# Memory cross-attention in float16 parts, its heads as generators, its output by pairs of heads

## The chip, the core and the metric

The kernel runs on one core of one Trainium2 chip. A core has five engines with instruction streams of their own: PE (TensorE, matrix multiplications; its weight loads are listed as PEld), DVE (VectorE), ACT (ScalarE), POOL (GpSimd) and SP (SyncE, which here issues most of the DMA transfers). Each stream is worked off in order, and an instruction waits for semaphores that other engines or transfers raise. The metric is the device time of one execution, in microseconds (us), as the median of repeated runs.

## What is computed

A trunk of two layers runs over 512 tokens of width 1024. Each layer has a mixing part (an RWKV-7 branch, a sparse-attention branch and gates, then one output projection `w_out`), a cross-attention into 256 memory tokens, and a feed-forward part: a SwiGLU in layer 0, eight experts of which each token takes two in layer 1 (MoE).

```python
x = x + memory_attention(rms_norm(x, norm_mem[l]), rms_norm(mem, mem_tok_norm[l]), mem_wq[l], ...)
h = rms_norm(x, norm_ffn[l])
# memory_attention: four heads of 128
q = rms_norm((h @ wq).reshape(bsz, seqlen, MEM_HEADS, MEM_HEAD_DIM), q_norm)
k = rms_norm(k.reshape(bsz, n_mem, MEM_HEADS, MEM_HEAD_DIM), k_norm)
s = jnp.einsum('bshd,bmhd->bhsm', q, k).astype(jnp.float32) * (MEM_HEAD_DIM ** -0.5)
p = jax.nn.softmax(s, axis=-1).astype(v.dtype)
```

Then p times v, and the heads side by side times `mem_wo`. The change touches this attention in both layers, and the step from it to the experts.

## The kernel before

Matrices are multiplied as pairs of float16 parts: a float32 operand a is split into hi (a cast to float16) and lo (a minus hi, in float16), and a product is three passes, hi·hi, lo·hi and hi·lo, added up in PSUM. `wtile` (L249 to L270) does this for a piece of weights of 512 KB: a DMA into a buffer `raw` on SP's queue (L259), the cast `whi` on ACT (L264), the rest `wlo` on DVE (L269). The buffers rotate in a pool set up with a number of raw, hi and lo buffers. `norm_T` (L182 to L202) normalises the four token tiles of 128 (square and sum on ACT L182, `rs` on DVE L164 and POOL L165, scaling on DVE L187), transposes them on PE (L193) and splits them (cast on ACT L201, lo on DVE L202). `proj_feat` (L286) and `proj_first` (L298) give outputs with features on the partitions, `proj_tok` (L328) with tokens on the partitions.

`mem_attn` (L1151 to L1217) takes the four heads one after the other: a projection `pf`, a copy `aqT` and a square of it, sums `pss`, scores `pms` (L1190), softmax (`amx`, exp into `apr`, its sum, and `apr` scaled at L1203), transposes `pmt` (L1209), and `pmo` (L1215), the product with v. The scores and `pmo` are float32 products there, of one pass each in the code, and `pmo` alone is split, into `oh` and `ol`. When all heads are there, `resid` (L1087 to L1093) multiplies by `mem_wo` in two halves of 512 columns over all four heads and adds to x. The keys and values of the memory tokens (`mem_kv`, L1106 to L1148) are made ahead: those of layer 0 at the start of the program, those of layer 1 inside the attention of layer 0, by the table `KV`, and kept in DRAM as `kTd` and `vd` in float32.

The weights of `w_out`, of the attention and of the FFN of layer 0 share one pool. The order of instructions on every engine comes from a scheduler that moves instructions of the text past one another where the data allow it; on SP it sets in which order the loads are issued. After `w_out` of layer 0, DVE's queue also holds seven small rows that prepare constants of layer 1's RWKV branch (`mu`, `w`, `a`, `kc`), which wait for DMAs of a few KB that stand behind the weight loads on SP.

In layer 1 the attention is followed by `norm_T` with rows that are kept (`row`), the splits `rowh` (ACT, L1281) and `rowl` (POOL, L1282), the router (transposes, `eh` and `el`, logits `plog`, then the choice on DVE) and the experts. Their first splits, `ewhi` (ACT, L1516) and `ewlo` (DVE, L1517), stand in the queues among the router's work. The experts' weights, 2 MB at a time, go into `eraw`, of which the pool `moeraw` holds four.

## Time and profile before

| what | us |
|---|---|
| median of 3 runs (lowest, highest) | 2107.54 (2106.56, 2109.30) |
| the profiled execution | 2112.5 |
| its span in the trace | 2110.7 |
| the stages in the trace: `w_out` of layer 0 | 524 to 566.3 |
| attention 0, with the keys and values of layer 1 | 566.3 to 669.6 |
| FFN of layer 0 | 669.6 to 1016 |
| mixing of layer 1, and its `w_out` | 1016 to 1553 |
| attention 1 | 1553 to 1629.9 |
| norm and router | 1629.9 to 1675 |
| experts | 1675 to 2098 |

The profiled execution was 5.0 us longer than the median, and 1.8 us of its time lie around the span. The page gives the busy time of the engines over the whole span (PE 93%) and in 40 slices. Stages differ, so the trace was read stage by stage: the busy time of each engine and the granted clock of TensorE in each stretch, and then, in order of time, what each engine did and what ended each idle time. The clock has two levels, 2.4 GHz (written 1.00) and 1.2 GHz (0.50). A busy time of one matmul in these rows reaches to its modelled end; how long PE needs for a row of matmuls is read from where the next ones start.

### The profile page before, as it was taken

To read this page: it belongs to the slowest core of one execution; us is meant where nothing else is said; L and a number is where in the kernel's file an instruction comes from. 1 tells how busy PE (TensorE), PEld (TensorE's weight loads), DVE (VectorE), ACT (ScalarE), POOL (GpSimd) and SP (SyncE) were. 2 spreads that over 40 slices of the span, in tenths; PEclk is the share of its full clock that TensorE was granted. 3 is DMA by queue.
4 is the path that set the end of the run, shared out by engine and by line. 5 is a ranking of instruction groups with operands and counts; after the bars stand their busy time and mean duration, and the time that the engine had idled before them with its cause. 6 is when DMAs were issued, how large, how long until landed. Compare 5 with 4: busy or idle time off the path is not lost.

```text
span 2110.7 us, 40673 instructions
## 1 busy us (share of the span) xinstructions
PE 1959.2 (93%) x16712; PEld 1291.7 (61%) x16712; DVE 1403.1 (66%) x2338; ACT 1018.8 (48%) x1641; POOL 343.5 (16%) x358
## 2 busy tenths in 40 slices
PE   7998899899999999999999888979998699999997
PEld 4664466364555444444583546536454699999996
DVE  6776987747655333322578997574755688888887
ACT  5543345443444333322543444543343588888883
POOL 2260601003000000000251350100200310000002
PEclk9998899979999999999999998988999799999998
DMA  7343424425551333333334332443544599999994
GB/s 230 104 98 78 120 68 127 107 79 164 170 150 50 110 100 100 102 107 101 117 82 98 80 114 63 110 103 110 165 129 171 164 377 372 352 353 345 346 348 135
DMA packets 346709, 332.51 MB, mean 158 GB/s; under 512 B 101889, under 2 KB 263809, under 8 KB 346514
## 3 DMA queue, kind: packets, MB, share of 16 engines
q1 hardware_dynamic: 335408, 306.03, 46.5%
q10 hardware_dynamic: 8482, 15.39, 2.0%
q0 software_dynamic: 2624, 8.40, 1.1%
q8 instruction: 133, 2.18, 0.4%
q14 instruction: 62, 0.51, 0.1%
HBM read 297.05 MB, written 32.72 MB: 156 GB/s over the span
## 4 chain that ended last, share of the span: by engine, by line
PE 68%; DVE 14%; DMA 6%; issue 3%; ACT 3%; SPq 2%; POOL 2%; ACTq 0%; DVEq 0%; POOLq 0%
PE pf L286 22%; PE pe L1534 11%; PE ptok L328 10%; PE py L1579 6%; PE pSy L901 3%; PE pf L298 2%; PE ptok L346 2%; DVE wlo L269 1%; DVE iacc L515 1%; DVE pr L1000 1%; DVE m L514 1%; PE psc L524 1%; ACT whi L264 1%; PE pp L555 1%; PE pA L805 1%
## 5 line engine op out<-in xcount | busy, mean ns | idle before, releaser
L264 ACT ACTIVATE whi<-raw 128x1024 f16<-128x1024 f32 (+3 forms) x242 | 227.2, 940 | 446.4 <-PE pf L286 193.4
L269 DVE SCALAR_TENSOR_TENSOR wlo<-raw,whi 128x1024 f16<-128x1024 f32 (+3 forms) x208 | 232.5, 1119 | 206.2 <-ACT whi L264 201.0
L1517 DVE SCALAR_TENSOR_TENSOR ewlo<-eraw,ewhi 128x1024 f16<-128x1024 f32 x265 | 321.1, 1221 | 61.9 <-ACT ewhi L1516 51.9
L286 PEld LDWEIGHTS <-whi 128*128 128x128 f16 x1888 | 184.5, 100 | 236.2 <-issue 39.2
L1516 ACT ACTIVATE ewhi<-eraw 128x1024 f16<-128x1024 f32 x265 | 277.5, 1053 | 80.6 <-PE py L1579 33.4
L1534 PE MATMUL pe<-XT,ewhi 128*128 128x144 f16 x2816 | 208.4, 227 | 2.4 <-issue 2.4
L1534 PEld LDWEIGHTS <-ewhi 128*128 128x128 f16 x2816 | 185.0, 98 | 3.6 <-issue 3.1
L286 PE MATMUL pf<-hh,whi 128*128 128x512 f16 x448 | 173.4, 387 | 2.4 <-ACT gt L1047 1.1
L286 PE MATMUL pf<-hl,whi 128*128 128x512 f16 x448 | 173.4, 387 | 0.0
L286 PEld LDWEIGHTS <-wlo 128*128 128x128 f16 x944 | 91.8, 99 | 112.8 <-issue 12.0
L286 PE MATMUL pf<-fh,whi 128*128 128x512 f16 x336 | 127.3, 379 | 0.0
L286 PE MATMUL pf<-fl,whi 128*128 128x512 f16 x336 | 127.3, 379 | 0.0
L1534 PE MATMUL pe<-XT,ewlo 128*128 128x144 f16 x1408 | 117.9, 227 | 1.0 <-issue 1.0
L286 PE MATMUL pf<-hh,wlo 128*128 128x512 f16 x448 | 113.4, 385 | 0.0
L267 POOL TENSOR_TENSOR wlo<-raw,whi 128x1024 f16<-128x1024 f32 (+3 forms) x34 | 58.5, 1721 | 288.5 <-ACT raw L266 199.1
L1579 PE MATMUL py<-HT,ewhi 128*128 128x144 f16 x1408 | 103.0, 226 | 0.1
L165 POOL TENSOR_TENSOR rs<-rs,nrm_e 128x1 f32<-128x1 f32 x28 | 16.8, 601 | 519.7 <-DVE rs L164 519.7
L1534 PEld LDWEIGHTS <-ewlo 128*128 128x128 f16 x1408 | 94.7, 98 | 1.6 <-issue 1.6
L1579 PEld LDWEIGHTS <-ewhi 128*128 128x128 f16 x1408 | 91.6, 98 | 0.3 <-issue 0.2
L286 PE MATMUL pf<-fh,wlo 128*128 128x512 f16 x336 | 79.4, 379 | 0.0
L346 PE MATMUL ptok<-whi,hh 128*128 128x256 f16 (+1 forms) x320 | 75.1, 275 | 2.1 <-ACT qe L482 2.0
L346 PE MATMUL ptok<-whi,hl 128*128 128x256 f16 (+1 forms) x320 | 75.1, 275 | 0.0
(459 smaller groups left out, 3934.2 us busy)
## 6 DMA issues: line engine op xcount, KB each, us to landing
raw<-in_w_in_dram SPq DMA_DIRECT2D x76, 512.0 KB
eraw<-in_moe_wg_dram SPq DMA_DIRECT2D x16, 2048.0 KB
eraw<-in_moe_wu_dram SPq DMA_DIRECT2D x16, 2048.0 KB
eraw<-in_moe_wd_dram SPq DMA_DIRECT2D x16, 2048.0 KB
eraw<-in_moe_wg_dram SPq DMA_DIRECT2D x8, 1536.0 KB
eraw<-in_moe_wu_dram SPq DMA_DIRECT2D x8, 1536.0 KB
eraw<-in_moe_wd_dram SPq DMA_DIRECT2D x8, 1536.0 KB
raw<-in_ffn_wg_dram SPq DMA_DIRECT2D x22, 512.0 KB
```

What stands on the lines that cost most here:

```text
L264: nc.scalar.activation(hi, raw, AF.Copy, scale=SW)
L267: nc.gpsimd.tensor_tensor(lo, raw, hi, OP.subtract)
L269: nc.vector.scalar_tensor_tensor(lo, raw, SW, hi, OP.mult, OP.subtract)
L286: self.nc.tensor.matmul(p, lhsT=w[:, k, :], rhs=x[k], start=first, stop=last)
L298: m = self.nc.tensor.matmul(ps[i][:, cs], lhsT=w[:, k, :], rhs=x[k][:, cs], start=hf == 0 and start, stop=stop, skip_group_check=True)
L328: mm(ps[t][:, :N], lhsT=x[:, k0 + k, ts], rhs=w[:, k, :], start=k0 == 0 and first, stop=k0 + kg == kt and last)
L346: mm(p, lhsT=x[:, k0 + k, ts], rhs=w[:, k, :], start=k0 == 0 and t % 2 == 0 and first, stop=k0 + kg == kt and last, skip_group_check=True)
L901: m = mm(p[e][:, cc % 4, jj, :], lhsT=l, rhs=r, start=first[e] is None, stop=x == (1 if cc else 0), skip_group_check=True)
L1516: a = nc.scalar.activation(r[0], w, AF.Copy, scale=SW)
L1517: d = nc.vector.scalar_tensor_tensor(r[1], w, SW, r[0], OP.mult, OP.subtract)
L1534: mm(p[:, i * n:(i + 1) * n], lhsT=w[:, k, :], rhs=XT[:, k, h, :], start=z == 0, stop=z == len(ms) - 1)
L1579: mm(ps[d], lhsT=w[:, i, d * P:(d + 1) * P], rhs=HT[:, k, h, :], start=k == 0 and w is wh and h == 0 and d % per == 0, stop=k == FT - 1 an ...
```

## The change

In `mem_attn`: queries, keys, values and probabilities are split into float16 parts, so that each score block is three passes of 128x256 where it was one float32 product, and `pmo` six passes of 128x512 where it was two float32 products. The splits are a cast on ACT and a subtraction on DVE each, where one copy stood; `kTd` and `vd` hold both parts. Each head is a generator with a pause in the middle; the second half of head h is written behind the first half of head h+2. The product with `mem_wo` is made for heads 0 and 1 and then for heads 2 and 3, so x is added to twice as often. The attention has a weight pool of its own (three raw, three hi, three lo), opened over free space, and `hold` orders its loads behind the last load of `w_out`. The normalised input lies in one tile with the tag "hl", no longer also in "hh". For the experts, the fourth raw buffer is a pool of its own; the router's split rows are allocated ahead of the row tiles; the last tile's `rowl` is on DVE, and its `rowh` is ordered behind the last `eh`.

```diff
     def split_ps(self, hi, lo, p, scale=None):
...
-            nc.scalar.copy(hi, p)
+            self.marks["hi"] = nc.scalar.copy(hi, p).ins
...
             self.lastw = nc.sync.dma_start(raw[:, :, o:o + n], pc.rearrange("(k p) c -> p k c", p=P)).ins
+            if self.hold:
+                self.order(self.lastw, self.hold)
...
-        hh = self.hp.tile([P, KT, SEQ], F16, name="qh", tag="hh", bufs=1)
-        hl = self.hp.tile([P, KT, SEQ], F16, name="ql", tag="hl", bufs=1)
-        self.norm_T(x, NT, [(I["norm_mem"][l], hh, hl)])
-        with tc.tile_pool(name="mattn", bufs=1, reuse_waits="tile") as mp:
+        hq = self.hp.tile([P, 2, KT, SEQ], F16, name="qhl", tag="hl", bufs=1)
+        hh, hl = hq[:, 0], hq[:, 1]
+        with self.more_weights(3, 3, 3), tc.tile_pool(name="mattn", bufs=1, reuse_waits="tile") as mp:
...
-                nc.vector.tensor_copy(qT, pq)
+                self.split_ps(qT[:, 0, :], qT[:, 1, :], pq, self.SM / SW)
...
-                        nc.tensor.matmul(psc[:, i * 256:(i + 1) * 256], lhsT=qT[:, t * P:(t + 1) * P], rhs=kT[:, h, :],
-                                         start=True, stop=True)
+                        for z, (a, b) in enumerate(three):
+                            nc.tensor.matmul(psc[:, i * 256:(i + 1) * 256], lhsT=qT[:, a, t * P:(t + 1) * P], rhs=kT[:, b, h, :],
+                                             start=z == 0, stop=z == 2)
...
-                for mt in range(2):
-                    nc.tensor.matmul(po, lhsT=v[:, mt, h * P:(h + 1) * P], rhs=pT[:, mt, :], start=mt == 0, stop=mt == 1)
-                self.split_ps(oh[:, h, :], ol[:, h, :], po)
-            self.resid(I["mem_wo"][l], oh, ol, x, 4)
+                    self.split_ps(pT[mt][:, 0, :], pT[mt][:, 1, :], pp, self.SP)
+                po = self.sm("pmo")
+                for z, (mt, (a, b)) in enumerate(itertools.product(range(2), ((0, 0), (0, 1), (1, 0)))):
+                    nc.tensor.matmul(po, lhsT=v[:, b, mt, h * P:(h + 1) * P], rhs=pT[mt][:, a, :], start=z == 0, stop=z == 5)
+                self.split_ps(oh[:, h, :], ol[:, h, :], po, 1 / (self.SM * self.SP))
+                yield
+            def output(pair, hf, kg=2):
+                hs, ks = slice(hf * 512, hf * 512 + 512), slice(2 * pair, 2 * pair + 2)
+                ps = self.proj_tok([I["mem_wo"][l][pair * 256:pair * 256 + 256, hs]], oh[:, ks, :], ol[:, ks, :], NT, 2, kg=kg)
+                for t in range(NT):
+                    nc.vector.scalar_tensor_tensor(x[:, t, hs], ps[t], 1 / SW, x[:, t, hs], OP.mult, OP.add)
+            wq = lambda h: I["mem_wq"][l][:, h * P:(h + 1) * P]
+            hs = [head(h, pq) for h, pq in enumerate(self.proj_first([wq(0), wq(1)], hk, lk))]
+            for g in hs:
+                next(g)
+            next(kv, None)
+            for h in (2, 3):
+                hs.append(head(h, self.proj_feat(wq(h), hk, lk)))
+                next(hs[h - 2])
+                next(hs[h])
+                for _ in range(2 if h == 2 else 0):
+                    next(kv, None)
+            output(0, 0)
+            next(hs[2])
+            output(0, 1)
+            next(hs[3])
+            output(1, 0, 1)
+            output(1, 1)
...
                 for t, r in enumerate(rows):
-                    self.marks["rows"] = nc.scalar.copy(hr[0][:, t, :], r).ins
-                    nc.gpsimd.tensor_tensor(hr[1][:, t, :], r, hr[0][:, t, :], OP.subtract)
+                    a = nc.scalar.copy(hr[0][:, t, :], r).ins
+                    (nc.vector if t == NT - 1 else nc.gpsimd).tensor_tensor(hr[1][:, t, :], r, hr[0][:, t, :], OP.subtract)
+                self.order(a, self.marks["hi"])
+                self.marks["rows"] = a
```

How the order of instructions moves is shown at three places. The first is the start of attention 0. On SP, behind the last loads of `w_out`, stood before:

```order
L259 DMA raw<-in_w_out_dram 128x2x512 x3
L259 DMA raw<-in_mem_wq_dram 128x8x128 x2
L259 DMA raw<-in_mem_wkv_dram 128x2x512 x8
L259 DMA raw<-in_mem_wq_dram 128x8x128 x2
L259 DMA raw<-in_mem_wo_dram 128x2x512 x4
```

and now:

```order
L259 DMA raw<-in_w_out_dram 128x2x512 x3
L259 DMA raw<-in_ffn_wg_dram 128x8x128
L259 DMA raw<-in_ffn_wu_dram 128x8x128
L259 DMA raw<-in_ffn_wg_dram 128x8x128
L259 DMA raw<-in_mem_wq_dram 128x8x128 x2
L259 DMA raw<-in_mem_wkv_dram 128x2x512
L259 DMA raw<-in_ffn_wu_dram 128x8x128
L259 DMA raw<-in_ffn_wg_dram 128x8x128
L259 DMA raw<-in_mem_wkv_dram 128x2x512 x3
```

Five loads of the FFN, which stood behind the whole attention, now stand among its first loads, three of them ahead of `mem_wq`. On ACT, from the squares of the first two token tiles on, stood before (`qh` is the hi part of the normalised input; the two `whi` rows are `mem_wq`'s):

```order
L182 ACTIVATE xs,ssq<-x 128x1024 x2
L264 ACTIVATE whi<-raw 128x1024
L1160 DMA akT<-kTd_174 128x1024
L1161 DMA av<-vd_175 128x1024
L201 CAST qh<-pT 128x4x128
L264 ACTIVATE whi<-raw 128x1024
L201 CAST qh<-pT 128x4x128
L182 ACTIVATE xs,ssq<-x 128x1024
L201 CAST qh<-pT 128x4x128 x2
L182 ACTIVATE xs,ssq<-x 128x1024
```

and now (the single `whi` rows are the FFN's, the `x2` row is `mem_wq`'s):

```order
L182 ACTIVATE xs,ssq<-x 128x1024 x2
L266 ACTIVATE whi<-raw 128x1024
L1169 DMA akT<-kTd_174 128x2048
L201 CAST qhl<-pT 128x4x128
L1170 DMA av<-vd_175 128x2048
L201 CAST qhl<-pT 128x4x128 x2
L182 ACTIVATE xs,ssq<-x 128x1024
L266 ACTIVATE whi<-raw 128x1024
L201 CAST qhl<-pT 128x4x128
L182 ACTIVATE xs,ssq<-x 128x1024
L266 ACTIVATE whi<-raw 128x1024 x2
```

The split of `mem_wq` on ACT has moved behind the squares of all four token tiles. Layer 1 has the same order on ACT, without the FFN's splits.

The second place is DVE in attention 0, where the constants of layer 1 stand. Before, they stood ahead of the copy `aqT` of a head's projection:

```order
L1195 SCALAR_TENSOR_TENSOR amx<-amx,aqs 128x2
L1200 RECIPROCAL asm<-asm 128x2
L1203 TENSOR_SCALAR apr<-apr,asm 128x256 x2
L591 TENSOR_SCALAR mu_9132<-mu 128x14
L623 TENSOR_SCALAR w_9255<-w_9255 128x4
L623 TENSOR_SCALAR a_9257<-a_9257 128x4
L592 TENSOR_SCALAR mu<-mu 128x14
L626 TENSOR_SCALAR kc_9271<-ka 128x4
L1173 COPY aqT<-pf 128x512
```

and now they stand in the last head's softmax:

```order
L1200 SCALAR_TENSOR_TENSOR amx<-amx,aqs 128x2
L594 TENSOR_SCALAR mu_9229<-mu 128x14
L205 SCALAR_TENSOR_TENSOR ol<-pmo,oh 128x512
L1199 TENSOR_REDUCE amx<-pms 128x2
L626 TENSOR_SCALAR w_9352<-w_9352 128x4
L595 TENSOR_SCALAR mu<-mu 128x14
L626 TENSOR_SCALAR a_9354<-a_9354 128x4
L1205 RECIPROCAL asm<-asm 128x2
L1200 SCALAR_TENSOR_TENSOR amx<-amx,aqs 128x2
L1208 TENSOR_SCALAR apr<-apr,asm 128x256 x2
```

They have moved from the middle of the attention to its last head. The third place is ACT in the router of layer 1. From the third tile's `rowh` on stood before:

```order
L1281 CAST rowh<-row_15166 128x1024
L201 CAST eh<-pT 128x4x128 x3
L189 DMA hd<-row_15188 128x1024
L1281 CAST rowh<-row_15188 128x1024
L1516 ACTIVATE ewhi<-eraw 128x1024 x2
L201 CAST eh<-pT 128x4x128
L1516 ACTIVATE ewhi<-eraw 128x1024 x3
L201 CAST eh<-pT 128x4x128
```

and now:

```order
L1312 CAST rowh<-row_15357 128x1024
L201 CAST eh<-pT 128x4x128 x3
L189 DMA hd<-row_15379 128x1024
L201 CAST eh<-pT 128x4x128 x2
L1312 CAST rowh<-row_15379 128x1024
L1549 ACTIVATE ewhi<-eraw 128x1024 x5
```

The last two `eh` now stand ahead of the last `rowh` and of all five `ewhi`.

## Rows read from the trace of the kernel before

**Rows 1.** By stage: length, busy PE, PEld, DVE, ACT, POOL; clock, DMA share, GB/s

```profile
566.30:669.60 103.30, 93.91 (x491) 55.88 (x490) 60.80 (x119) 44.59 (x83) 9.16 (x10) 0.95 0.39 112
669.60:1016.00 346.40, 344.26 (x1658) 162.38 (x1657) 121.29 (x134) 104.60 (x127) 2.84 (x6) 1.00 0.35 105
1553.00:1629.90 76.90, 68.59 (x385) 42.38 (x383) 42.17 (x91) 28.45 (x62) 5.59 (x9) 1.00 0.47 163
1629.90:1675.00 45.10, 24.74 (x272) 21.55 (x273) 29.71 (x88) 24.54 (x40) 20.55 (x16) 0.75 0.42 127
...
1690.00:2054.00 364.00, 364.00 (x5696) 362.72 (x5694) 314.24 (x318) 294.15 (x366) 18.52 (x15) 1.00 0.98 357
```

**Rows 2.** Groups of PE's matmuls in attention 1: busy, mean ns | idle before, releaser

```profile
L1215 PE MATMUL pmo<-apT,av 128*128 128x512 f32 x16 | 8.4, 618 | 2.4 <-ACT apT L1213 2.4
...
L1209 PE MATMUL pmt<-ct,apr 128*128 128x128 f32 x32 | 4.9, 280 | 2.6 <-DVE apr L1203 2.6
```

**Rows 3.** PE in order of time, attention 1: start us, us, operation [idle before]

```profile
1577.79 0.38 PE L286 MATMUL pf<-qh,whi 128*128 128x512 f16 x1
...
1581.03 0.38 PE L286 MATMUL pf<-ql,whi 128*128 128x512 f16 x1
...
1587.29 1.02 PE L1215 MATMUL pmo<-apT,av 128*128 128x512 f32 x2
1588.15 1.03 PE L1190 MATMUL pms<-akT,aqT 128*128 128x256 f32 x4
1589.01 0.81 PE L328 MATMUL ptok<-whi,oh 128*128 128x512 f16 x3
```

**Rows 4.** Start of attention 0, in order of time: PE, ACT and DVE

```profile
566.32 1.91 PE L193 MATMUL pT<-ct,xs 128*128 128x128 f32 x16
570.54 0.38 PE L298 MATMUL pf<-qh,whi 128*128 128x256 f16 x2 [2.32 <-ACT qh L201]
...
564.84 1.06 ACT L264 ACTIVATE whi<-raw 128x1024 f16<-128x1024 f32 x1 [1.63 <-issue]
...
568.39 0.58 ACT L201 CAST qh<-pT 128x512 f16<-128x512 f32 x1
568.86 1.07 ACT L182 ACTIVATE xs<-x 128x1024 f32<-128x1024 f32 x1
...
571.73 1.27 DVE L187 SCALAR_TENSOR_TENSOR xs<-x,rs,gb 128x1024 f32<-128x1024 f32 x1
```

**Rows 5.** Middle of attention 0, in order of time: DVE and PE

```profile
624.53 0.18 DVE L591 TENSOR_SCALAR mu<-mu 128x14 f32<-128x14 f32 x1 [2.25 <-DMA mu<-in_rwkv_mu_dram]
...
627.84 0.41 PE L328 MATMUL ptok<-whi,oh 128*128 128x512 f16 x1 [3.65 <-ACT aq L1174]
```

**Rows 6.** Busy time and granted clock behind two gaps of PE (columns as in Rows 1)

```profile
628.00:639.00 11.00, 10.34 (x28) 6.40 (x27) 3.69 (x13) 1.90 (x5) 1.01 (x1) 0.53 0.31 91
1553.00:1560.00 7.00, 4.34 (x38) 3.73 (x37) 6.50 (x10) 5.07 (x9) 0.62 (x2) 1.00 0.88 283
```

**Rows 7.** Start of attention 1, in order of time: PE

```profile
1553.03 1.91 PE L193 MATMUL pT<-ct,xs 128*128 128x128 f32 x16
...
1557.26 0.38 PE L298 MATMUL pf<-qh,whi 128*128 128x256 f16 x2 [2.32 <-ACT qh L201]
...
1557.98 0.27 PE L298 MATMUL pf<-ql,whi 128*128 128x256 f16 x1 [0.35 <-DVE ql L202]
```

**Rows 8.** Router, in order of time: POOL, DVE, PE, ACT

```profile
1639.05 7.28 POOL L1282 TENSOR_TENSOR rowl<-row,rowh 128x1024 f16<-128x1024 f32 x3
...
1639.11 3.14 DVE L187 SCALAR_TENSOR_TENSOR row<-x,rs,gb 128x1024 f32<-128x1024 f32 x1
...
1642.39 1.94 PE L193 MATMUL pT<-ct,row 128*128 128x128 f32 x8 [1.99 <-DVE lg L1370]
...
1648.82 0.57 ACT L201 CAST eh<-pT 128x512 f16<-128x512 f32 x1
```

**Rows 9.** Who waits for whom among the experts (1690 to 2054), SP's DMA queue: total, times, longest

```profile
SPq L1497 <- DVE ewlo L1517: 120.9, 14, 10.3
```

More of the change, by code (lines that the diff above doesn't have):

```diff
@@ L272 @@
     nsplit = 0
+    hold = None
     share = 1 << 30
@@ L309, in order, with proj_tok @@
                                                                        mybir.DependencyReason.DATA), reason="order")
-    def proj_tok(self, pieces, xh, xl, nt, kt=KT, tail=1, tag="acc"):
+    def proj_tok(self, pieces, xh, xl, nt, kt=KT, tail=1, tag="acc", kg=None):
         N = sum(p.shape[1] for p in pieces)
-        kg = max(1, 1024 // N)
+        kg = kg or max(1, 1024 // N)
         while kt % kg:
@@ L1146, in mem_kv @@
                 nc.tensor.transpose(pt[:, h * P:(h + 1) * P], kn[:, h, :], self.ident)
[L1147 removed]
+            self.split_ps(*[kT[:, i, :, t * P:(t + 1) * P] for i in range(2)], pt.rearrange("p (h t) -> p h t", h=4))
         nc.scalar.dma_start(kTd, kT)
         yield
+    SM = 8.0
     def mem_attn(self, l, x, kv):
         nc, I, tc = self.nc, self.I, self.tc
[L1154 to L1159 removed]
+        hq = self.hp.tile([P, 2, KT, SEQ], F16, name="qhl", tag="hl", bufs=1)
+        hh, hl = hq[:, 0], hq[:, 1]
+        with self.more_weights(3, 3, 3), tc.tile_pool(name="mattn", bufs=1, reuse_waits="tile") as mp:
+            oh = mp.tile([P, 4, SEQ], F16, name="oh")
+            ol = mp.tile([P, 4, SEQ], F16, name="ol")
+            self.norm_T(x, NT, [(I["norm_mem"][l], hh, hl)])
+            kT = mp.tile([P, 2, 4, 256], F16, name="akT")
+            v = mp.tile([P, 2, 2, 512], F16, name="av")
+            three = ((0, 0), (1, 0), (0, 1))
             nc.scalar.dma_start(kT, self.kTd[l])
@@ L1162, in mem_attn, with head @@
             hk, lk = [hh[:, k, :] for k in range(KT)], [hl[:, k, :] for k in range(KT)]
-            oh = mp.tile([P, 4, SEQ], F16, name="oh")
-            ol = mp.tile([P, 4, SEQ], F16, name="ol")
-            wq = lambda h: I["mem_wq"][l][:, h * P:(h + 1) * P]
-            pqs = self.proj_first([wq(0), wq(1)], hk, lk)
-            for h in range(4):
-                for _ in range(self.KV[h]):
-                    next(kv, None)
-                pq = pqs[h] if h < 2 else self.proj_feat(wq(h), hk, lk)
-                qT = mp.tile([P, SEQ], F32, name="aqT", bufs=2)
-                q2 = mp.tile([P, SEQ], F32, name="aq2", bufs=2)
-                nc.vector.tensor_copy(qT, pq)
+            def head(h, pq):
+                qT = mp.tile([P, 2, SEQ], F16, name="aqT", bufs=2)
+                q2 = mp.tile([P, SEQ], F32, name="aq2", bufs=1)
+                self.split_ps(qT[:, 0, :], qT[:, 1, :], pq, self.SM / SW)
                 nc.scalar.activation(q2, pq, AF.Square)
@@ L1203, in mem_attn @@
                         nc.vector.tensor_scalar(pr[:, t, :], pr[:, t, :], sm[:, t:t + 1], None, OP.mult)
-                po = self.sm("pmo")
-                pT = mp.tile([P, 2, SEQ], F32, name="apT", bufs=2)
+                yield
+                pT = [mp.tile([P, 2, SEQ], F16, name="apT", tag=f"apT{i}", bufs=2) for i in range(2)]
                 for mt in range(2):
@@ L1263, in moe @@
             cx.enter_context(c2)
+            raw1 = c2.enter_context(tc.tile_pool(name="moeraw1", bufs=1, side="right", reuse_waits="tile"))
             xp = c2.enter_context(tc.tile_pool(name="moex", bufs=2, reuse_waits="tile"))
@@ L1644 @@
     INV = 300
-    KV = (1, 2, 0, 0)
     WB = ((2, 3, 3), (2, 3, 3), (2, 3, 3), (0, 5, 5))
@@ L1706, in layer @@
             self.resid(I["w_out"][l], *mh, x, KT)
+            self.hold = self.lastw
             bx.close()
@@ L1710, in layer @@
                 self.mem_attn(l, x, kv)
+                self.hold = None
         if l % 2:
             c2 = ExitStack()
-            rawp = c2.enter_context(tc.tile_pool(name="moeraw", bufs=self.RAWS, side="right", reuse_waits="tile"))
+            rawp = c2.enter_context(tc.tile_pool(name="moeraw", bufs=self.RAWS - 1, side="right", reuse_waits="tile"))
             self.mem_attn(l, x, kv)
+            self.hold = None
             px.close()
```

26 lines of the change are left out of this document (11 added, 15 removed).

## The prediction, made before the changed kernel was run

> **What bounds the kernel now.** I read the busy time by stage first, to see which engine each stage waits for [rows 1]. In the FFN of layer 0 PE is busy for 344.26 of 346.40 us, among the experts for 364.00 of 364.00. There PE is the bound, and a stage in front of them that ends earlier moves the rest forward whole. In the two attentions PE is busy for 93.91 of 103.30 and 68.59 of 76.90 us and no other engine for more than 60.80, so PE is the bound with holes in it. In the router PE has 24.74 of 45.10 us at a mean clock of 0.75: a chain of small steps through ACT, DVE and POOL. Second, PE in order of time, for what sets its rate and who ends its idle times. 16 starts of 128x512 float16 matmuls, from 1577.79 to 1581.03, are 0.216 us apart [rows 3]; a modelled busy time of 0.38 says nothing of that. Third, what stood in the queue of the engine that ended each hole.
>
> **The products.** In the rows a float32 product is two records. Four `pms` records, that is scores of two token tiles, take from 1588.15 to 1589.01, 0.86 us; two `pmo` records, half a head, from 1587.29 to 1588.15, also 0.86 [rows 3]. The new scores are three passes of 256 columns, at half of 0.216 each: 6 x 0.108 = 0.65 for two tiles, so a head drops from 1.72 to 1.30. The new `pmo` is six passes of 0.216, 1.30 against 1.72. That is 0.84 us a head, 3.4 an attention, on PE and so on the path. Against it stand splits: per head one more cast on ACT for `aqT`, one more for `apT`, and two-operand subtractions on DVE in place of copies. A cast took 0.58 [rows 4]; DVE has 60.80 busy us in 103.30 and 42.17 in 76.90 [rows 1], so I cost them at nothing as long as PE has another head's projection or output to do. The cover is gone in the last head; there I leave 2 us of waits (below).
>
> **Attention 0, the middle.** Before, DVE's queue came to the constants of layer 1 while their loads were still under way: it idled 2.25 us for `mu` and shortly again for others, with the copy `aqT` behind them, ACT's square behind that and PE behind the square. PE idled 3.65 us until 627.84 [rows 5], and then ran 11 us at a granted clock of 0.53 [rows 6], 1.2 GHz for most of it: 11.00 x 0.47 = 5.2 us lost. Sum 8.9. In the new order the same rows stand in the last head's softmax, with the same SP loads ahead of them (they follow all weight loads of the attention), so the wait comes back there: DVE's 2.25 and the short ones behind it, of which I take 2.5 in all on the path, since outputs of heads 0 and 1 are there for PE in part. Bounds: 0, if all is covered; 8.9 again, if PE idles as long as it did. Net gain 6.4, bounds 0 to 8.9.
>
> **The small holes.** In attention 1, PE waits before `pmo` for ACT's copy of the probabilities, 2.4 us in all, and before `pmt` for DVE's scaling, 2.6 [rows 2]: 5.0. Each of these eight or so holes also hides about 0.2 us behind the modelled end of the matmul before it (0.38 against 0.216 [rows 3]): 1.6, so 6.6. With the second half of a head behind the scores of the head after next, PE has passes to do in all of them but the last. Followed through with these durations, the new order leaves about 2 us, before `pmo` of head 0 and of head 3. Gain 4.6 in attention 1, and I take 2.5 in attention 0, whose holes were partly filled by the keys and values of layer 1. Bounds 0 and 6.6 each: the scheduler interleaved the heads before too (a `pmo` stands beside the next head's `pms` in rows 3), so less may be left to win.
>
> **The starts.** Here the change costs. In attention 0 PE ended the transposes of two tiles at about 568.1 and began `pf` at 570.54 [rows 4]. Now a third tile's transposes stand ahead of `pf`, and they need its scaling, which before ended at 571.73 + 1.27 = 573.0 and, with ACT's square at about 568.7, can end at 571.7. ACT then has an FFN `whi` (1.06), a cast (0.58), the last tile's square (1.07 and its read) and only then `whi` of `mem_wq` (1.06) [rows 4]: 573.1 to 573.9. So `pf` starts 2.6 to 3.4 us later, with 0.9 us of transposes done in the meantime: 1.7 to 2.5 lost, I take 2. In attention 1 the same order without the FFN's splits gives `pf` at 1560.0, where it ran from 1557.98 on [rows 7]; less the third tile, 1.4 lost; bounds 0.5 to 3.
>
> **The clock at the starts.** PE would now stand still from 568.1 to 571.7 or later, 3.6 us, and from 1554.9 to 1559.1, 4.2 us. The trace has a gap of 3.65 us with the clock at 0.53 behind it, and one of 2.32 and 0.35 us, with two matmuls between, after which it stayed at 1.00 [rows 5 to 7]. My gaps are nearer to the first. What follows here is dense projection work, so I take half of the 5.2 us for the two places together, 2.6; bounds 0 and 2 x 5.2. The Trainium skill (TensorE: Matmul & The Clock Gate, Part 1: The HAM clock gate) says that the half-rate clock is the default and that only recent activity keeps it away; by that alone both gaps would cost, and the sum would be about 2.6 us smaller. The rows agree that such gaps can cost and leave open that these do.
>
> **The FFN behind it, and the loads.** Five FFN loads and three FFN splits now come early. They leave the FFN's own start: before, the first `pf` there came after two `whi` that stood among the norm's casts; worth about one cast, 0.6, an estimate [rows 4]. The FFN is bound by PE, so fewer loads in it are worth nothing. On SP they stand ahead of `mem_wq` and of seven `mem_wkv` loads; DMA is at a share of 0.39 in that stage [rows 1], so I cost the queueing at nothing beyond the start. The accumulations into x double (eight more on DVE), covered by the passes of the next output block.
>
> **Router.** The last tile's transposes ended at 1642.39 + 1.94 = 1644.3, but its second `eh` began at 1648.82, behind five `ewhi` and a `rowh` on ACT [rows 8]. Now it stands ahead of them: 4.5 us earlier. DVE gets that tile's `rowl`, ahead of the last logits: `rowh` must come first (1.04 more on ACT), about 1.0 us lost. The five `ewhi` come later but are needed only at the first expert. Gain 3.5; bounds 1.6 and 4.5. While POOL did three `rowl` (7.28 us), DVE's scaling of a tile took 3.14 us instead of 1.27 [rows 4, 8]. POOL's would be over by about 1644, before DVE's `rowl`. The Trainium skill (GPSIMD Engine Reference, 1. Specifications) says that GpSimd shares its SBUF interfaces with VectorE and that instructions with two SBUF inputs contend; DVE's `rowl` is one, and if POOL were late the gain would be 1.6.
>
> **Experts.** PE never waits there, and SP waits for buffers (120.9 us for one group of loads alone [rows 9]), so the DMA share of 0.98 is not the bound yet. Were it, the loads start earlier by as much as the router ends earlier, so the gain would still pass.
>
> **Sum.** Attention 0: 3.4 + 6.4 + 2.5 - 2.0 + 0.6 = 10.9. Attention 1: 3.4 + 4.6 - 1.4 = 6.6. Router 3.5. Clock -2.6. Together 18.4. The profiled execution would go from 2112.5 to 2094.1; it lay 5.0 above the median of 2107.54, so I expect a median of 2089.1.
>
> **Rivals.** (1) The waits move and do not go: the constants cost as much in the last head, the heads were already interleaved, and both start gaps drop the clock. What is left is 6.8 of passes, 3.5 of router and 0.6, plus half of the waits' terms ((6.4 + 2.5 + 4.6) / 2 = 6.75), less starts of 3.4 and the clock twice, 5.2: 9, so 2098.5. For it: the new tail has one head's softmax with the least work beside it. Against: heads 0 and 1 have about 10 us of output passes free there. (2) More goes: the clock holds at both starts, and the router's half clock shrinks with its chain. 18.4 + 2.6 + 2.5 for the constants + 3 = 26.5, so 2081. (3) Slower than before: the loads of attention 0. Five FFN loads of 512 KB stand in front of or among thirteen weight loads, and the second `mem_wq` load waits for PE's last use of `w_out`'s operand; everything behind it on SP waits too. If each weight piece then comes late by the time of one load, which I put at 3 us, between PE's gaps of 2.32 and 3.65 [rows 5, 7], seven late pieces eat the 18.4; at nine the kernel takes 2089.1 + 27 = 2116. It decides when PE's waits name a DMA of `raw` in attention 0. Against: DMA share 0.39. (4) The scheduler's other order in the mixing of layer 1, which the diff does not mean to touch, takes the gain back: SP, POOL and DVE differ there in a few dozen rows. 18.4 us would need two stalls like the 3.65 us one with its clock loss, 8.9 each; then about 2107.
>
> **Chances.** Forecast (2082 to 2095) 0.52, rival 1 (2095 to 2102) 0.23, rival 2 (below 2082) 0.15, rival 4 or a mix near no change 0.05, rival 3 0.05. Leaving out the far ends gives 2078 to 2101. Less than 0.2%, 4.2 us, can hardly be told from no change: faster by more 0.90, within 0.05, slower 0.05.
>
> **What would show it.** Right: `pms` as 256-column passes 0.108 apart; attention 0 in about 93 us and attention 1 in about 70; no idle time of PE over 3 us after the starts; the last `eh` about 14.5 us behind the end of attention 1 instead of 19. Wrong: PE's clock at 0.5 behind 573 and 1560; DVE idle for `mu` in the last head with PE idle beside it; PE waiting for `raw` loads; the mixing of layer 1 longer than 505 us.

## The result, and the profile after

The changed kernel took 2079.98 us (median of 4 runs, 2075.39 to 2081.22), the kernel before beside it 2108.42 (4 runs, 2106.56 to 2110.37): a ratio of 0.9861, 95% interval 0.9843 to 0.988. It is faster by 28 us, 10 more than the sum said: inside the outer range (2078 to 2101) and 2 below the band of the forecast (2082 to 2095). The profiled execution is the fastest of the four, 2075.39 us with a span of 2073.6.

The busy time by stage of the changed kernel answers [rows 1]; the columns are the same. The stretches are attention 0, the FFN of layer 0, the mixing of layer 1 (from the last FFN matmul to the first of `w_out`), attention 1, and from there to the first expert's first `pe`:

```profile
563.80:660.10 96.30, 88.74 (x513) 53.66 (x512) 68.79 (x136) 48.67 (x92) 8.55 (x9) 0.95 0.43 126
660.10:1010.10 350.00, 347.89 (x1665) 164.06 (x1664) 122.02 (x135) 106.21 (x128) 5.52 (x8) 1.00 0.34 102
1010.10:1484.20 474.10, 438.71 (x3471) 267.55 (x3470) 351.83 (x714) 214.51 (x422) 125.25 (x135) 0.95 0.38 103
1526.00:1597.70 71.70, 65.50 (x409) 42.81 (x408) 50.02 (x105) 34.30 (x73) 6.62 (x9) 0.95 0.51 176
1597.70:1629.00 31.30, 18.86 (x175) 16.55 (x174) 27.13 (x80) 20.40 (x35) 10.59 (x8) 0.62 0.49 170
```

Of the kernel before, the same view for the two stretches that [rows 1] cuts elsewhere, the mixing of layer 1 and the way from attention 1 to the first `pe`:

```profile
1017.20:1510.50 493.30, 445.06 (x3471) 270.46 (x3470) 357.06 (x711) 215.23 (x423) 131.17 (x136) 0.93 0.36 98
1629.50:1663.80 34.30, 17.41 (x174) 15.08 (x173) 26.29 (x78) 20.31 (x35) 12.62 (x9) 0.70 0.45 155
```

From the last `w_out` matmul to the last of `mem_wo`, attention 0 went from 103.1 to 96.3 and attention 1 from 76.7 to 71.7; the router went from 34.3 to 31.3. The largest piece lies where the diff touches nothing: the mixing of layer 1 went from 493.3 to 474.1, with the same 3471 matmul records on PE. PE's idle time there fell from 48.2 to 35.4 us; the rest goes with the clock, 0.93 before and 0.95 now.

**Start of attention 0** (answers [rows 4]). PE, ACT, DVE in order of time, and PE's busy time and clock there:

```profile
564.03 1.91 PE L193 MATMUL pT<-ct,xs 128*128 128x128 f32 x16
569.64 1.94 PE L193 MATMUL pT<-ct,xs 128*128 128x128 f32 x8 [3.70 <-DVE xs L187]
571.38 1.91 PE L301 MATMUL pf<-qhl,whi 128*128 128x256 f16 x8
...
569.62 2.14 ACT L266 ACTIVATE whi<-raw 128x1024 f16<-128x1024 f32 x2
...
568.21 1.28 DVE L187 SCALAR_TENSOR_TENSOR xs<-x,rs,gb 128x1024 f32<-128x1024 f32 x1 [0.73 <-POOL rs L165]
...
571.00:581.00 10.00, 10.00 (x68) 7.63 (x67) 7.37 (x10) 3.75 (x6) 1.40 (x1) 0.81 0.85 258
```

`pf` begins 7.35 us after the first transposes, where it was 4.22 before; the gap is 3.70, and the clock behind it is 0.81 over 10 us.

**Last head of attention 0** (answers [rows 5] and [rows 6]), DVE and PE in order of time, and the stretch behind:

```profile
634.14 0.17 DVE L594 TENSOR_SCALAR mu<-mu 128x14 f32<-128x14 f32 x1 [3.12 <-DMA mu<-in_rwkv_mu_dram]
634.23 0.68 DVE L205 SCALAR_TENSOR_TENSOR ol<-pmo,oh 128x512 f16<-128x512 f32 x1
...
634.97 0.39 PE L331 MATMUL ptok<-whi,ol 128*128 128x512 f16 x1 [2.62 <-DVE ol L205]
...
630.00:640.00 10.00, 7.38 (x34) 3.96 (x33) 6.58 (x22) 4.23 (x12) 0.62 (x1) 0.83 0.63 108
```

The wait for `mu` is there again, now with `ol` behind it, and PE behind `ol`; the clock falls again.

**Attention 1** (answers [rows 2], [rows 3] and [rows 7]): the start, its clock, then scores of two token tiles and the one hole over 1 us that is left in the heads.

```profile
1531.95 1.94 PE L193 MATMUL pT<-ct,xs 128*128 128x128 f32 x8 [3.87 <-DVE rs L164]
...
1530.00:1536.00 6.00, 4.05 (x19) 3.38 (x20) 5.51 (x7) 4.95 (x7) 1.82 (x2) 0.54 0.65 205
...
1557.95 0.82 PE L1195 MATMUL pms<-akT,aqT 128*128 128x256 f16 x6
1558.61 0.59 PE L289 MATMUL pf<-qhl,whi 128*128 128x512 f16 x2
...
1563.95 0.59 PE L1218 MATMUL pmo<-apT,av 128*128 128x512 f16 x2 [1.49 <-ACT apT L204]
```

Six score passes take 1558.61 - 1557.95 = 0.66 us, 0.110 each.

**The mixing of layer 1.** PE's largest difference there lies in the RWKV branch's chain of 64x64 products (`pH`, copied to `UV`, then `pMQ`, `pSy`). PE, ACT and DVE of the kernel before, in order of time, and 30 us of that stretch:

```profile
1263.39 1.15 PE L873 MATMUL pH<-H,TT 64*64 64x64 f32 x32 [1.82 <-ACT AM L848]
1264.37 1.04 PE L882 MATMUL pMQ<-AM 64*64 64x128 f32 x16
1265.96 1.09 PE L882 MATMUL pMQ<-AM 64*64 64x128 f32 x16 [0.55 <-ACT AM L848]
...
1271.13 3.68 PE L882 MATMUL pMQ<-AM 64*64 64x128 f32 x32 [3.87 <-ACT UV L848]
...
1270.50 0.58 ACT L848 COPY UV<-pH 64x512 f32<-64x512 f32 x1 [3.51 <-DVE UV L847]
...
1266.90 0.68 DVE L514 MAX8 m<-iacc 128x8 f32<-128x512 f32 x1
...
1269.20 0.68 DVE L515 MATCH_REPLACE8 iacc<-m,iacc 128x512 f32<-128x512 f32 x1
1269.79 0.67 DVE L847 COPY UV<-pH 64x512 f32<-64x512 f32 x1
...
1264.40:1294.40 30.00, 24.11 (x166) 16.27 (x161) 27.74 (x73) 11.05 (x32) 0.00 (x0) 0.77 0.13 36
```

The same place of the changed kernel:

```profile
1248.07 1.15 PE L876 MATMUL pH<-H,TT 64*64 64x64 f32 x32
1249.05 1.92 PE L885 MATMUL pMQ<-AM 64*64 64x128 f32 x32
...
1251.83 1.67 PE L289 MATMUL pf<-hh,wlo 128*128 128x512 f16 x7
1253.43 1.96 PE L885 MATMUL pMQ<-AM 64*64 64x128 f32 x32
...
1249.00 0.69 DVE L517 MAX8 m<-iacc 128x8 f32<-128x512 f32 x1
1249.62 0.66 DVE L850 COPY UV<-pH 64x512 f32<-64x512 f32 x1
...
1245.80:1275.80 30.00, 30.00 (x264) 20.20 (x264) 29.22 (x78) 16.64 (x44) 0.00 (x0) 1.00 0.18 54
```

DVE is nearly full in both. `UV` is copied in two halves, here ACT's after DVE's. `pMQ` reads `AM` and not `UV`: by the kernel's text it waits for the PSUM bank of `pH`, which is free when both halves are copied. Before, DVE's half of the second `UV` copy stood in its queue behind several rounds of the sparse branch's top-k (`MAX8`, `MATCH_REPLACE8`), ACT's half waited 3.51 us for it, PE stood still for 3.87 us, and the 30 us have a clock of 0.77. In the new order the copy follows `pH` after one `MAX8`, projection passes fill the time to the next `pMQ`, and PE is busy for 30.00 of 30.00 us at full clock. Counted by equal numbers of PE records, from record 1350 to record 1950 of the stage, PE needed 92.2 us before and 80.8 after: 11.4 of the 19. In the second executions of both kernels (`before_again` and `after_again`, below) it needed 89.4 and 81.7.

**Router** (answers [rows 8]), ACT and DVE in order of time:

```profile
1612.51 0.59 ACT L201 CAST eh<-pT 128x512 f16<-128x512 f32 x1 [0.27 <-PE pT L193]
...
1607.24 3.14 DVE L187 SCALAR_TENSOR_TENSOR row<-x,rs,gb 128x1024 f32<-128x1024 f32 x1
...
1614.07 1.22 DVE L1313 TENSOR_TENSOR rowl<-row,rowh 128x1024 f16<-128x1024 f32 x1
```

The last `eh` begins 14.8 us behind the end of attention 1, where it was 19.3.

### The profile page after: what moved, and what is told of

Same layout as the page of the kernel before. It is cut to its first block, busy times and chain, and to the rows that moved or that the text cites. A ratio compares the mean times of both kernels' runs of the same rounds, so it can differ in the third digit from the quotient of the medians.

```text
span 2073.6 us, 40817 instructions
## 1 busy us (share of the span) xinstructions
PE 1940.1 (94%) x16760; PEld 1286.0 (62%) x16760; DVE 1413.4 (68%) x2373; ACT 1029.1 (50%) x1661; POOL 341.0 (16%) x357
## 4 chain that ended last, share of the span: by engine, by line
PE 70%; DVE 12%; DMA 7%; ACT 3%; issue 3%; POOL 3%; SPq 2%; DVEq 0%; ACTq 0%; POOLq 0%
PE pf L289 23%; PE ptok L331 12%; PE pe L1567 10%; PE py L1612 6%; PE pSy L904 3%; PE pf L301 3%; PE ptok L349 2%; PE psc L527 1%; DVE wlo L271 1%; DMA eraw<-in_moe_wd_dram 1%; DVE iacc L518 1%; DVE pr L1003 1%; PE pA L808 1%; PE pT L193 1%; PE pp L558 1%
## 5 line engine op out<-in xcount | busy, mean ns | idle before, releaser
L266 ACT ACTIVATE whi<-raw 128x1024 f16<-128x1024 f32 (+2 forms) x244 | 227.7, 934 | 436.9 <-PE pf L289 187.3
L271 DVE SCALAR_TENSOR_TENSOR wlo<-raw,whi 128x1024 f16<-128x1024 f32 (+2 forms) x210 | 232.0, 1107 | 201.7 <-ACT whi L266 190.3
L349 PEld LDWEIGHTS <-hh 128*128 128x128 f16 x640 | 62.4, 100 | 15.5 <-issue 8.2
```

The costliest lines, as they stand in the source:

```text
L266: nc.scalar.activation(hi, raw, AF.Copy, scale=SW)
L271: nc.vector.scalar_tensor_tensor(lo, raw, SW, hi, OP.mult, OP.subtract)
L349: mm(p, lhsT=x[:, k0 + k, ts], rhs=w[:, k, :], start=k0 == 0 and t % 2 == 0 and first, stop=k0 + kg == kt and last, skip_group_check=True)
```

## The experiments

Stage lengths are read from the profiled execution of each kernel: attention from the last `w_out` matmul to the last of `mem_wo`, the mixing as above.

**Which part of the change gives what.** Four kernels built from both texts: `before_again` has the old attention in both layers and the old router, `att0` the new attention in layer 0 alone, `att1` in layer 1 alone (the keys and values that attention 0 makes for it are in float16 there), `router` only the router's part. The fourth raw buffer has its own pool in `att1` and `router`.

```diff
+    NEW = (1, 0)     # att0; (0, 1) att1; (0, 0) router and before_again
+    def mem_attn(self, l, x, kv):
+        if not self.NEW[l]:
+            self.hold = None
+        (self.mem_attn_new if self.NEW[l] else self.mem_attn_old)(l, x, kv)
```

> The kernel before once more, the same program, for how far two profiled executions of one program differ stage by stage. Theory O (order): the mixing of layer 1 was shorter after the change because the scheduler put its instructions in another order; then this run has the mixing of before, from the first transposes of layer 1 to the first w_out matmul 493 us (1017.6 to 1510.5) within 5. Theory S (spread): stages of one program vary by 10 us and more between executions; then it may as well be 480. Time 2108 by both.

> Only layer 0's attention and its keys and values as in the changed kernel; layer 1's attention, the router and the raw buffers as before. The order of PE and POOL in the mixing of layer 1 is word for word that of the changed kernel. Theory O: attention 0 gives 7, the mixing 12 to 20, so 2081 to 2089. Theory S: only the 7, so 2101.

> Only layer 1's attention as in the changed kernel (its keys and values are made in float16 parts inside the old attention 0, and the fourth raw buffer has its own pool); attention 0 and the router as before. The mixing of layer 1 stands in a third order. Attention 1 itself gains 5 (76.9 to about 72). Theory S: 2103. Theory O: the mixing may fall on either side, 493 plus or minus 20, so 2083 to 2123, and its time in the profile is more than 5 us off 493.

> Only the router's part: split rows ahead of the row tiles, the last tile's rowl on DVE, its rowh behind the last eh, the fourth raw buffer in its own pool. PE, ACT, DVE and POOL stand as before up to the router. The last eh comes 4.5 us earlier, the first expert matmul 3 us; the experts themselves as before or up to 3 us shorter. Time 2102 to 2105 by both theories.

| kernel | median us | ratio (95%) | attention 0 | FFN gate, up | mixing of layer 1 | attention 1 | to first `pe` |
|---|---|---|---|---|---|---|---|
| before | 2108.83 | 1 | 103.1 | 234.0 | 493.3 | 76.7 | 34.3 |
| before_again | 2110.26 | 0.9993 (0.9968 to 1.0018) | 103.6 | 234.0 | 496.2 | 76.7 | 34.3 |
| att0 | 2086.26 | 0.9889 (0.9855 to 0.9923) | 95.8 | 235.1 | 476.4 | 81.5 | 34.4 |
| att1 | 2094.18 | 0.9933 (0.9909 to 0.9957) | 104.0 | 234.6 | 487.3 | 70.8 | 33.9 |
| router | 2108.99 | 1.0001 (0.9981 to 1.0021) | 106.4 | 234.0 | 494.2 | 76.7 | 31.1 |

`before_again` and `router` have the order of `before` in the mixing, row for row on PE, ACT, DVE and POOL, and its length within 3 us; `att0` has the changed kernel's order, row for row on PE and POOL, and 476.4, though its attention 1 and its router are the old ones. `att1` has a third order and 487.3. So the mixing goes with the order in which the scheduler put it, not with chance and not with what runs behind it. No kernel here changes the order of this stage alone, so what else comes with a new order, such as the place of its buffers, is not ruled out. In `router` the 3.87 us stop stands at the same step as before:

```profile
1272.03 3.25 PE L885 MATMUL pMQ<-AM 64*64 64x128 f32 x28 [3.87 <-ACT UV L851]
```

In `att0` PE's largest stop from 1226 to 1256 is 1.24 us, and none is at `pMQ`. `router` gains 3.2 up to the first `pe`; its median, expected at 2102 to 2105, shows no gain, and its interval leaves room for 4 us to either side. Behind the first `pe`, PE waits 2.38 us for the first gathered rows, where `before_again` had 1.05. `before` had no such wait and still took longer from there to the first output of an expert (`pyt`), so this wait alone does not settle where the gain goes. From the end of attention 1 to the first `pyt`, the ten traces with the new router in this document have 90.4 to 96.0 us, mean 93.6, the four with the old one 93.5 to 98.2, mean 95.1. Of `router`, then of `before_again`, PE in order of time:

```profile
1697.60 1.97 PE L1456 MATMUL pxt<-ct,xrows 128*128 128x128 f32 x8 [2.38 <-DMA xrows<-hd,idxB]
```

```profile
1699.82 1.09 PE L1451 MATMUL pxt<-ct,xrows 128*128 128x128 f32 x8 [1.05 <-DMA xrows<-hd,idxB]
```

**Products or structure.** `f16only` has the float16 parts in the old order of heads, with the old pool and one output at the end; `f32pipe` has generators, pool and output by pairs with float32 products.

```diff
-            hs = [head(h, pq) for h, pq in enumerate(self.proj_first([wq(0), wq(1)], hk, lk))]
...
+            for h in range(4):
+                for _ in range(self.KV[h]):
+                    next(kv, None)
+                pq = pqs[h] if h < 2 else self.proj_feat(wq(h), hk, lk)
...
+            self.resid(I["mem_wo"][l], oh, ol, x, 4)
```

```diff
-                        for z, (a, b) in enumerate(three):
-                            nc.tensor.matmul(psc[:, i * 256:(i + 1) * 256], lhsT=qT[:, a, t * P:(t + 1) * P], rhs=kT[:, b, h, :],
-                                             start=z == 0, stop=z == 2)
+                        nc.tensor.matmul(psc[:, i * 256:(i + 1) * 256], lhsT=qT[:, t * P:(t + 1) * P], rhs=kT[:, h, :],
+                                         start=True, stop=True)
```

> The attention of before (heads one after the other in the text, one output over four heads, the shared weight pool) with queries, keys, values and probabilities in float16 parts; router and raw pool as in the changed kernel. The stages are measured from the last w_out matmul to the last one with mem_wo: before 103.1 and 76.7 us, changed 96.3 and 71.8. Theory P (the passes count one for one, 3.4 us an attention): 99.7 and 73.3. Theory Q (the splits on ACT and DVE eat it, the pipelining does it all): 103 and 76.7. The mixing of layer 1 stands in a fourth order: 474 to 496.

> The changed kernel with its generators, pairs, own weight pool and hold, but queries, keys, values and probabilities in float32 as before (the product of one pass in the code). Theory P: the attentions take 3.4 us more than in the changed kernel, 99.7 and 75.2. Theory Q: 96.3 and 71.8. Mixing in a fifth order: 474 to 496.

`f16only`: median 2089.42, ratio 0.9911 (0.9885 to 0.9937), attention 0 99.8, attention 1 73.9, mixing 479.3; its profiled execution was the fastest of ten, 8 below its median. `f32pipe`: 2099.14, 0.9947 (0.9924 to 0.9971), 97.2, 73.0, mixing 495.2. The parts alone save 3.3 and 2.8 us in the two attentions, near the 3.4 of the sum. The structure alone saves 5.9 and 3.7. Together they save 6.8 and 4.9, so the parts add only 0.9 and 1.2 on top of the structure (0.7 and 2.5 if `after_again`, below, is taken for the changed kernel). PE's gaps are the same with both products, 3.70 and 3.87 us at the starts and 2.63 and 2.62 in the last head of attention 0; that the shorter products are partly spent in such waits fits this, but is not shown. Each has an order of its own in the mixing, 479 and 495 us long.

**The pool and the starts.** `nopool` leaves the attention in the shared pool, without `hold`. `start` orders the splits of `mem_wq`'s first two blocks on ACT ahead of the last two squares and casts of the norm, and lets the FFN's early loads follow `mem_wo`'s.

```diff
-        with self.more_weights(3, 3, 3), tc.tile_pool(name="mattn", bufs=1, reuse_waits="tile") as mp:
+        with tc.tile_pool(name="mattn", bufs=1, reuse_waits="tile") as mp:
```

```diff
+                if t > 1 and self.early:
+                    self.order(sq, self.early)
...
+            ws = [self.wtile([wq(i)], KT) for i in range(2)]
+            self.early = self.whis[-2]
...
-                self.hold = None
+                self.hold = self.lastw
```

> The changed kernel without the attention's own weight pool and without hold, so that its weights load through w_out's buffers as before. Theory W (the late starts come from the pool and hold, which put the split of mem_wq behind the squares of all tiles): the first projection matmul comes about 4.2 us behind the last w_out matmul as before, not 7.6, the clock stays at full speed there, and the attentions take 92 and 67. Rival: two raw buffers make the loads late in the middle, PE waits for raw or whi there, and the attentions take 96 and 72 or more. Mixing in a sixth order.

> The changed kernel with two orders added: ACT splits the first piece of mem_wq ahead of the casts of the normalised input and of the squares of tiles 2 and 3, and the FFN's first loads stand behind mem_wo's. PE then has the projection of two tiles between the transposes of tiles 1 and 2. Theory G (each start loses 1.4 to 2 us of waiting and 2.6 of half clock): attention 0 about 91 and attention 1 about 67 instead of 96.3 and 71.8. Rival: the wait only moves behind the first projection matmuls, to tiles 2 and 3, and the attentions stay within 1.5 us. Mixing in a seventh order; without its part the kernel is 9 us faster than the changed one by G, the same by the rival.

`nopool`: 2095.82, 0.9931 (0.9905 to 0.9958); attention 0 96.7, attention 1 69.1, mixing 494.5. `start`: 2088.41, 0.9903 (0.9879 to 0.9927); 94.9, 68.7, mixing 491.0. Both starts come down to gaps as before or shorter, and attention 1 gains 2.7 and 3.1 by it. In attention 0 a stop of PE eats the rest: 3.30 us in `nopool`, again by the constants, and 3.31 in `start`, where the constants' rows on DVE wait for nothing. There it is `start`'s own second order. DVE stands 5.39 us before the `wlo` of an FFN weight, whose cast on ACT waits 4.78 us for its load, now issued behind `mem_wo`'s; behind that `wlo` stands `aqs`, for which PE waits. Of `nopool`, the `pf` row of both starts and the stop; then of `start`, the same of attention 0, with DVE and ACT:

```profile
567.85 0.59 PE L301 MATMUL pf<-qhl,whi 128*128 128x256 f16 x2 [2.32 <-ACT qhl L201]
...
633.31 0.61 PE L331 MATMUL ptok<-whi,ol 128*128 128x512 f16 x1 [3.30 <-DVE ol L205]
...
1551.36 0.38 PE L301 MATMUL pf<-qhl,whi 128*128 128x256 f16 x2 [2.32 <-ACT qhl L201]
```

```profile
565.92 1.80 PE L307 MATMUL pf<-qhl,whi 128*128 128x256 f16 x15 [1.35 <-DVE qhl L206]
...
628.00 1.12 PE L1224 MATMUL pmt<-ct,apr 128*128 128x128 f32 x4 [3.31 <-DVE aqs L1194]
...
626.64 1.23 DVE L275 SCALAR_TENSOR_TENSOR wlo<-raw,whi 128x1024 f16<-128x1024 f32 x1 [5.39 <-ACT whi L270]
...
625.56 1.06 ACT L270 ACTIVATE whi<-raw 128x1024 f16<-128x1024 f32 x1 [4.78 <-DMA raw<-in_ffn_wg_dram]
```

**The changed kernel again, the start in its own order, and the constants by themselves.** `s1` has the mend of `start` in layer 1 alone, which leaves the order of the mixing as it is on PE, POOL and SP. `c` puts DVE's rows for layer 1's constants behind the last accumulation of attention 0. `c_s` has that and the mend of both starts.

```diff
+            self.early = self.whis[-2] if l else None
```

```diff
+        late = lambda i: self.order(i.ins, self.marks["wo"]) if l else None
+        late(nc.vector.tensor_scalar(mu1, mu, -1 / SW, 1 / SW, OP.mult, OP.add))
+        late(nc.vector.tensor_scalar(mu, mu, 1 / SW, None, OP.mult))
...
+                    self.marks["wo"] = nc.vector.scalar_tensor_tensor(x[:, t, hs], ps[t], 1 / SW, x[:, t, hs], OP.mult, OP.add).ins
```

> The changed kernel once more, as it stands. By the theory that the order of a program's instructions sets the length of its mixing of layer 1, this stage is again 472 to 477 us from the last FFN matmul to the first matmul of w_out (474.0 before), attention 0 is 96 to 97, attention 1 is 71 to 73, and the ratio to the kernel before is 0.984 to 0.988. By the rival that the 19 us were a matter of that one execution, the mixing comes out anywhere between 475 and 496.

> The changed kernel, and in layer 1 alone both splits of mem_wq's first two blocks stand on ACT ahead of the last casts and squares of the norm, so that the first projection does not wait for them. The order of the mixing's instructions on PE, POOL and SP is the changed kernel's, row for row. Theory (order): mixing 472 to 477, as in the changed kernel, where the run with the same fix in both layers had 491.0 in another order. Theory (start of attention 1 costs 3 by its gap of 3.87 and the clock behind it): attention 1 goes from 71.8 to 68.5 to 69.0, attention 0 stays 96 to 97, and the time is about 3 below the changed kernel's, a ratio of 0.985. Rival: the mixing depends on what comes behind it, and is over 485; then the time is 12 or more above the changed kernel's.

> The changed kernel, and DVE's instructions on layer 1's constant rows stand behind the last accumulation of attention 0 into x, instead of in the last head. Theory (the constants cost their gap of 2.62 and the clock that falls behind it, 0.83 over 10 us): attention 0 goes from 96.3 to 92 to 93. Rival (the last head's chain is late anyway): the gap before the last head's output stays at 1.5 or more, attention 0 at 95 or more. The mixing of layer 1 comes in an order of its own: between 474 and 496 by theory, with no forecast inside this; so the time is -4 to +18 against the changed kernel, and the stage is what is read.

> The changed kernel with both mends: the splits of mem_wq's first two blocks ahead of the last casts and squares in both layers, and the constant rows of layer 1 behind attention 0. Theory: attention 0 is 90 to 92 (96.3 less 1.4 for the start, less 2.62 and about 1.7 of clock), attention 1 is 68.5 to 69.0; this would be what the prediction had for attention 0 (92.2) and 1 (70.1). Rival: another wait takes the constants' place, attention 0 stays at 94 or more. Mixing of layer 1 between 474 and 496, again in an order of its own.

| kernel | median us | ratio (95%) | attention 0 | FFN gate, up | mixing of layer 1 | attention 1 |
|---|---|---|---|---|---|---|
| after_again | 2082.29 | 0.9837 (0.9812 to 0.9862) | 96.5 | 236.0 | 479.2 | 70.5 |
| s1 | 2082.38 | 0.9835 (0.9809 to 0.9862) | 96.4 | 236.0 | 480.0 | 68.7 |
| c | 2096.20 | 0.9908 (0.9886 to 0.9929) | 91.0 | 235.3 | 495.0 | 70.6 |
| c_s | 2097.64 | 0.9916 (0.9895 to 0.9937) | 91.8 | 235.3 | 501.6 | 68.7 |

The mixing in the changed kernel's order is now measured four times: 474.1, 476.4, 479.2, 480.0, mean 477.4. The two last are over the 477 that was expected: the spread inside one order is 6 us, not 3. The order of before gave 493.3, 494.2, 496.2, mean 494.6. The difference, 17, stays well outside the spread. PE's idle time in the stage is 34 to 38 us in the four, and 45 to 49 in the three.

`c` settles the constants: with their rows out of the last head, attention 0 falls from 96.5 to 91.0, below the expected 92 to 93. Not all of the 5.5 is theirs. 0.8 is there by the 40th of the attention's 512 PE records: the start has the same gap of 3.70, but the clock came back sooner behind it. From the 400th record to the end PE needs 28.8 and 28.9 us in the two traces of the changed kernel and 24.3 in `c` and in `c_s`, so the constants cost 4.5. The FFN behind is 0.7 shorter in `c`, but not shown to be so by them: `att0` has their stop (2.97 us) and 235.1. PE's stretch over the last head, which had 0.83 of the clock, is at full rate:

```profile
627.00:643.00 16.00, 15.45 (x91) 8.94 (x90) 12.27 (x27) 7.12 (x16) 1.01 (x1) 1.00 0.45 82
```

`s1` brings attention 1 to 68.7 at full clock, as expected, but its median is the changed kernel's; the expected 3 us are not seen in the time, whose intervals of 0.26%, 5.5 us, to either side leave room for them. In `c_s` the mend of the start of attention 0 brought nothing: gaps of 1.41 and 2.13 us replaced the one of 3.70, and the clock fell behind them. PE there, and the stretch:

```profile
570.07 3.36 PE L307 MATMUL pf<-qhl,whi 128*128 128x256 f16 x15 [2.13 <-DVE qhl L206]
...
570.00:576.00 6.00, 5.93 (x32) 4.26 (x32) 5.33 (x8) 2.30 (x4) 1.06 (x2) 0.57 1.08 309
```

`c` and `c_s` have the best pair of attentions (91 and 69 to 71 us) and lose all of it in the mixing, 495.0 and 501.6. So no kernel here beats the changed one: what might is attention 0 of `c` with the mixing in the changed kernel's order, and that was not tried.

## Why the prediction was right or wrong

The direction holds. That the time lies in the outer range is luck: the sum does not hold by its own terms. To even out single executions, the stages of `before` and `before_again` are averaged here, and those of the changed kernel and `after_again`. The spans differ by 31.1 us: attention 0 7.0, the FFN -2.0, the mixing of layer 1 18.1, attention 1 5.6, from there to the first expert's first output (`pyt`) 1.8, the rest 0.7. The parts that the sum spoke of come to 7.0 - 2.0 + 5.6 + 1.8 = 12.4, where it had 18.4; the mixing, which it left out, gave more than all of them. Without it the time would have been about 2107.5 - 12.4 = 2095.1, where the forecast's band ends and rival 1's begins. Of the signs of being wrong, two came: the clock fell behind both starts, and DVE stood idle for `mu` in the last head with PE idle beside it.

- **The mixing of layer 1: the step that failed.** The prediction saw that the scheduler had ordered this stage otherwise and made it rival 4, with one sign only: that it takes the gain back. A new order can as well take stalls away. `router` against `att0` shows it is the order (494.2 and 476.4), and the rows around `pMQ` show where 8 to 11 of the 17 to 19 us arise: a copy on DVE's full queue moved ahead of top-k rounds whose result is needed later. For the rest no row is shown. Nor is this stop what makes every other order long: `f32pipe` and `c_s` pass the same 600 records in 82.5 and 83.2 us, near the changed kernel's 80.8, and lose their time elsewhere in the stage. The term needed bounds on both sides, and rows of before had the second one: a stop of 3.87 us and a clock of 0.77 over 30 us stand there to be counted as what another order may save. Why the scheduler found that order is not shown.
- **Products.** Right alone (3.3 and 2.8 measured for 3.4 each), too much as a term beside the others (0.7 to 0.9 and 1.2 to 2.5); that time saved between waits is partly waited away is argued, not shown.
- **Constants of layer 1.** The place was right, the size was not. I took 2.5 for their return in the last head, since outputs of heads 0 and 1 would be there for PE. DVE waited 3.12 us for `mu`, PE 2.62 behind it, the clock fell, and `c` and `c_s` price all of it at 4.5. With 8.9 before, by the one trace that the prediction had, the net gain was 4.4, not 6.4.
- **Small holes.** Of attention 1's waits before `pmo` and `pmt`, 5.0 in all [rows 2], one of 1.49 is left, and of 2.8 in attention 0, 0.6; with the start mended (`s1`) the stage is 68.7, 8.0 below before, where 3.4 + 4.6 = 8.0 was the sum without the start.
- **The starts.** The gaps came as worked out, 3.70 for 3.6 and 3.87 for 4.2. In attention 1 the start cost 70.5 or 71.8 less 68.7, 1.8 to 3.1, for 1.4 and half of 2.6 predicted. In attention 0 `pf` is 3.1 later with 0.9 of transposes done, 2.2 for 2.0, and a clock of 0.81 over 10 us is 1.9 more. That the clock falls behind both was the other half of the clock's term. The rule of the Trainium skill that was weighed there (TensorE: Matmul & The Clock Gate, Part 1: The HAM clock gate), that the half rate is the default and activity releases it, agrees: the clock was 0.81 over 10 us behind the one gap and 0.54 over the 6 us around the end of the other.
- **The FFN.** Put at +0.6, it was -2.0: its gate and up stage went from 234.0 to 236.0. The four traces with 236.0 us or more (both of the changed kernel, `s1`, `nopool`) have a stretch at half rate soon behind the start of the stage, 0.83 over its first 10 us in the changed kernel; the others, 234.0 to 235.3, have none, 1.00 in `c`. That is 0.7 to 0.9; where the other 1.1 comes from was not tried.
- **Router.** 3.2 up to the first `pe` for 3.5, by the steps named (last `eh` at 14.8 for 14.5). At the first `pyt` 1.8 is left, 1.5 by the means of all traces, both within the spread of the stretch, and `router`'s median shows no gain. The prediction had let it pass whole.
- **Rivals.** Rival 1 is half true: half of the constants' price came back in the last head (4.5 of 8.9) and both starts lose clock; but the small holes went. Rival 2 has the measured time in its band, but not by its reasons: the clock held at neither start, the constants came back, and the router's clock was 0.62, lower than the 0.70 before. Rival 3 falls: no wait of PE in attention 0 names a load of `raw`. Rival 4 came with the other sign.

## What to carry to other kernels

When a scheduler orders the whole program, a local change is also a new draw for every stage that shares its queues: nine orders of one unchanged stage, seven of them traced once, took from 474 to 502 us, more than the edit itself was worth. So compare the order of the untouched stages too, take the stalls that the trace shows there as bounds to both sides, and hold that order fixed when an edit is to be measured. A wait that is moved behind other work is gone only if DVE's (or ACT's) queue has nothing behind it that PE needs soon.
